# A two-layer decoder trunk in split fp32: the down projections as seven products of halves, the residual kept with tokens on the partitions

## The chip, the cores and the metric

One Trainium2 chip, one of its cores. The metric is the device time of one launch in microseconds (us); lower is better. The kernel before takes 1899.91 us, the median of 3 runs (1899.79 to 1900.06).

## The reference

Two layers, each a feed-forward part, a mixing part and a second feed-forward part, on 512 tokens of width 1024, in float32:

```python
D_MODEL = 1024; SEQ = 512; DEPTH = 2; D_FF = 2816
POOL_WINDOWS = (2, 4, 8, 16)     # four pool groups of 128 channels
HEAD_DIM = 64; N_Q_HEADS = 8; N_KV_HEADS = 2; WINDOW = BLOCK = 128

def swiglu(h, w_gu, w_down):
    g, u = jnp.split(h @ w_gu, 2, axis=-1)
    return (jax.nn.silu(g) * u) @ w_down

for l in range(DEPTH):
    x = x + 0.5 * swiglu(rmsnorm(x, ln_ffn1[l]), w_ffn1_gu[l], w_ffn1_down[l])
    h = rmsnorm(x, ln_mix[l])
    u_pool, q, k, v, gate_logits = jnp.split(h @ w_in[l], splits, axis=-1)
    a = pool_mixer(u_pool, pool_w[l], pool_scale[l]) @ w_pool_branch[l]
    b = swa_sink_attention(rope(norm(q)), rope(norm(k)), v, sinks[l]) @ w_attn_branch[l]
    g_pool, g_attn = jnp.split(jax.nn.sigmoid(gate_logits), 2, axis=-1)
    x = x + (g_pool * a + g_attn * b) @ w_out[l]
    x = x + 0.5 * swiglu(rmsnorm(x, ln_ffn2[l]), w_ffn2_gu[l], w_ffn2_down[l])
```

## The kernel before

**Arithmetic.** Every operand of a large product is split into a high part of type fp32r and a rest (`hi`, `lo`), and a product is three matmuls: hi with hi, hi with lo, lo with hi (`term`). The function `split` makes the pair: ScalarE (ACT) copies with rounding, VectorE (DVE) subtracts. Weights come in chunks of up to 1024 columns (`raw`, seven buffers) by DMA; `W.prep` is called after each half product and makes `wh` (ACT) and `wl` (DVE) of chunks ahead of use, up to four (`HI`) and three (`LO`) chunks ahead. All instructions run in the order in which the program writes them, on each engine: `keep_in_program_order`. All of them are issued from one helper line, so the profile gives one line number, L95, for nearly everything, and groups are told apart by the names of their tiles.

**A feed-forward part (`ffn`).** The 2816 hidden columns are 22 tiles of 128, in three groups of 8, 8 and 6 tiles. A group is two blocks of gate and up products (`block`, 512 or 384 columns of each) and then its part of the down product (`down`). A block forms its gate and up by seven products of half size in place of eight, named a11, s1, s2, s3, a12, s4, a22 after the weights they use; the weights move, the activations (`xgh`, `xgl`, in the combinations B11, T1 to T4, B21, B22) are stationary. Sums of weights come from accumulating DMAs on GpSimd's queue and from DVE (`sums`). Results `r` (first half of the tokens) and `v` (second half) have tokens on the partitions; `turned` transposes them on TensorE (PE) and splits them into the hidden operand `hh`, `hl`. The very first block (`plain`) uses no such products.

**Down, before.** For each of the eight output tiles `m` of 128 columns, the weights are stationary and the hidden operand moves: 8 (or 6) hidden tiles by 3 matmuls of 512 columns into one PSUM bank; `done` adds half of it to the residual `x`, held with features on the partitions (`[128, 8, 512]`). In the last group of a part, `done` also feeds the next norm: `nxt.split(m)` and `nxt.square(m)`. The norm's factor is applied behind the product (`rstd`), from a sum of squares that four matmuls with a column of ones (`sums`) form; in the mixing part it is spread over all partitions as `R`.

**The mixing part (`mix`).** It computes u (the pool input), q, k, v, the gates and the two branches, then `out`, again tile by tile with features on the partitions. Short chains of DVE, ACT and PE work (pool windows, the attention of the heads) are `stages` that run between the large products at places listed in tables (`NORMS`, `HEADS`, `ATT`, `POOL`).

**PSUM, before.** Eight banks of 512 columns. Each accumulator is a tile of one bank: six for the blocks and the down products, `pt_tp` and `pt_pv` for transposes; in `mix` four for products and a pair for scores.

Of the kernel before, what the change touches and what calls it, by code (L numbers as in the profile page):

```python
# [28 lines left out]
HALVES = (0, 4, 1, 5, 2, 6, 3, 7)  # L29
# [77 lines left out]
def trunk(ctx, tc, xT, consts, vecs, rows, w_g4, w_g3, w_d8, w_d6, w_qkv, w_u, w_pool, w_gate, w_br, w_out, out):  # L107
# [12 lines left out]
    x = xp.tile([P, KT, S], F32, name="x")  # L120
# [7 lines left out]
    pw = pa.tile([P, S], F32, name="pt_pv")  # L128
    for _ in range(WARM):
        nc.tensor.matmul(pw[:, :2 * P], warm[:, :P], warm, start=True, stop=True)  # L130
# [26 lines left out]
    class Weights:  # L157
# [3 lines left out]
        def __init__(self):  # L161
# [3 lines left out]
            for l in range(L):  # L165
                for f in range(2):
                    if f == 1:
                        for kind, src, n in (("u", w_u[l], 2), ("qkv", w_qkv[l], 6), ("u", w_u[l, 2:], 2),
                                             ("gate", w_gate[l], 2 * KT), ("br", w_br[l], KT)):
                            for i in range(n):  # L170
                                self.add(kind, CH, src[i])
                        for m in HALVES:
                            self.add("out", CH, w_out[l, m])
                    plain = l == f == 0
                    for gi, (at, group) in enumerate(groups(plain)):
                        for i, n in enumerate(group):
                            w = w_g4[l, f, (at - 768) // 512 + i] if at else w_g3[l, f, i]
                            if plain and gi == i == 0:
                                for j in range(2):
                                    for c in range(4):  # L180
                                        self.add("plain", 2 * n, w[j, c])
                            else:
                                self.block(w, 2 * n, FIRST if 2 * gi + i == int(plain) else ORDER)
                        for m in (HALVES if f == 1 and gi == 2 else range(KT)):
                            w = w_d8[l, f, at // 1024, m] if at else w_d6[l, f, m]
                            self.add("dn", sum(group), w)
# [8 lines left out]
        def block(self, w, n, order):  # L195

            at, name, first = len(self.plan), {}, len(self.loads)
            src = {"a11": (w[0], None), "s1": (w[1], w[1, 2:]), "s3": (w[0], w[1]), "a12": (w[0, 2:], None),
                   "a22": (w[1, 2:], None), "s2": (None, None), "s4": (None, None)}
            for k in order:  # L200
                for c in range(2):
                    s, m = src[k]
                    name[k, c] = self.add(k, n, None if s is None else s[c], None if m is None else m[c])
# [108 lines left out]
    bank = {}  # L312

    def mm():
        return bank["mm"].tile([P, S], F32, name="mm")
# [16 lines left out]

    class Norm:
# [5 lines left out]
        def split(self, k, between=lambda: None):  # L339

            g = self.gain[:, k:k + 1]
            if self.h is None:
                self.h = xl.tile([P, 7 * 4 * HT], F32R, name="xgh")
                self.l = xl.tile([P, 7 * 4 * HT], F32R, name="xgl")
                self.spare = [t[:, KT * S:] for t in (self.h, self.l)]
                if self.halves:
                    self.h, self.l = (t.rearrange("p (i k t) -> p i k t", i=7, k=4) for t in (self.h, self.l))
                else:
                    self.h, self.l = (t[:, :KT * S].rearrange("p (k t) -> p k t", k=KT) for t in (self.h, self.l))
            if not self.halves:  # L350
                split(self.h[:, k, :], self.l[:, k, :], x[:, k, :], scale=g, between=between)
            elif k < 4:
                split(*self.of(B11, k), halves(x[:, k, :])[:, 0:1, :], scale=g, between=between)
                self.first(k)
            else:
                xg = self.scaled(k)
                bh, bl = self.of(B21, k - 4, 2)
                nc.scalar.copy(out=bh, in_=halves(xg))
                between()
                self.others(k - 4, xg, lambda: nc.vector.tensor_tensor(  # L360
                    out=bl, in0=halves(xg), in1=bh.bitcast(F32), op=ALU.subtract
                ))

        def of(self, i, j, n=1):
            return [t[:, i:i + n, j, :] for t in (self.h, self.l)]

        def scaled(self, k):
            xg = temp("xg")
            nc.scalar.activation(out=xg, in_=x[:, k, :], func=AF.Copy, scale=self.gain[:, k:k + 1])
            return xg  # L370

        def first(self, j):
            d = temp("d")[:, :HT]
            nc.vector.tensor_tensor(out=d, in0=x[:, j, :HT], in1=x[:, j, HT:], op=ALU.subtract)
            split(*self.of(T1, j), halves(d), scale=self.gain[:, j:j + 1])

        def others(self, j, xg, between=lambda: None):
            t, u = temp("t23"), temp("t4")[:, :HT]
            gj = self.gain[:, j:j + 1]
            nc.vector.scalar_tensor_tensor(  # L380
                out=t[:, HT:], in0=x[:, j, HT:], scalar=gj, in1=xg[:, HT:], op0=ALU.mult, op1=ALU.subtract
            )
            nc.vector.scalar_tensor_tensor(
                out=t[:, :HT], in0=x[:, j, :HT], scalar=gj, in1=t[:, HT:], op0=ALU.mult, op1=ALU.subtract
            )
            nc.vector.tensor_tensor(out=u, in0=xg[:, :HT], in1=t[:, :HT], op=ALU.subtract)
            between()
# [3 lines left out]
        def split_plain(self, k, b12):  # L391
            g = self.gain[:, k:k + 1]
            if self.h is None:
                self.h, self.l = (
                    xl.tile([P, 7 * 4 * HT], F32R, name=n).rearrange("p (i k t) -> p i k t", i=7, k=4)
                    for n in ("xgh", "xgl")
                )
            if k < 4:
                split(*self.of(B11, k), halves(x[:, k, :])[:, 0:1, :], scale=g)
                split(*(t[:, k:k + 1, :] for t in b12), halves(x[:, k, :])[:, 1:2, :], scale=g)  # L400
            else:
                split(*self.of(B21, k - 4, 2), halves(x[:, k, :]), scale=g)

        def square(self, k):
            if self.acc is None:
                self.acc = xp.tile([P, S], F32, name="ssq")
                nc.scalar.activation(out=self.acc, in_=x[:, k, :], func=AF.Square)
            else:
                sq = temp("sq")
                nc.scalar.activation(out=sq, in_=x[:, k, :], func=AF.Square)  # L410
                nc.vector.tensor_tensor(out=self.acc, in0=self.acc, in1=sq, op=ALU.add)

        def sums(self, pt=None):
            if pt is None:
                pt = pa.tile([P, S], F32, name="pt_tp")
            for b in range(NB):
                nc.tensor.matmul(
                    pt[:, b:b + 1], self.acc[:, b * P:(b + 1) * P], ones[:, 0:1], start=True, stop=True
                )
            v = sp.tile([P, NB], F32, name="rs_v")  # L420
            nc.vector.tensor_scalar(
# [4 lines left out]
            if self.halves:  # L426
                return
# [7 lines left out]
        def spread(self):  # L435
            pr = pa.tile([P, S], F32, name="pt_pv")
# [8 lines left out]

    @with_exitstack
    def ffn(ctx, nm, nxt, last):
        hp = ctx.enter_context(tc.tile_pool(name="hp", bufs=1, reuse_waits="tile"))
        ep = ctx.enter_context(tc.tile_pool(name="ep", bufs=1, reuse_waits="tile"))
        sums = ctx.enter_context(tc.tile_pool(name="sums", bufs=2, reuse_waits="tile"))  # L450
        bank["mm"] = ctx.enter_context(tc.tile_pool(name="pf", bufs=6, space=PSUM, reuse_waits="tile"))
# [9 lines left out]
        turns = []  # L461

        def block(n, base, hid, order):
# [3 lines left out]
            pt = {}  # L467

            def product(i, b, kind, go):
                first = b not in pt  # L470
                if first:
                    pt[b] = [mm()[:, :n] for _ in range(2)]
                for c in range(2):
                    wh, wl = (t[:, :2 * n].rearrange("p (k f) -> p k f", k=2) for t in W.take(kind))
                    for q in range(2):
                        for k in range(2):
                            ah, al = (t[:, i, 2 * c + k, q * P:(q + 1) * P] for t in (nm.h, nm.l))
                            for j, (s, m) in enumerate(((ah, wh), (ah, wl), (al, wh))):
                                nc.tensor.matmul(
                                    pt[b][q], s, m[:, k, :], start=first and c == k == j == 0,  # L480
                                    stop=c == k == 1 and j == 2, skip_group_check=True,
                                )
                    if c == 0:
                        W.prep()
                if kind == order[1]:
                    turn()
                after = go() if go else None
                if kind == order[0]:
                    turn()
                W.prep()  # L490
                if after:
                    after()

            def each(make):
                return [make(q) for q in range(2)]

            new = lambda name: [ep.tile([P, 512], F32, name=f"{name}{q}")[:, :n] for q in range(2)]
            r1, sa, u2, v = {}, {}, {}, {}
# [561 lines left out]
```

## Time and profile before

| | before |
|---|---|
| median of 3 runs (lowest to highest) | 1899.91 us (1899.79 to 1900.06) |
| the profiled execution, from first to last instruction | 1899.3 us |
| PE matmul busy | 1890.0 us, 9072 matmuls |
| DVE busy | 1293.7 us |
| ACT busy | 840.3 us |
| GpSimd (POOL) busy | 83.1 us |
| moved by DMA | 256.10 MB |

The page lists, for each engine, the time in which an instruction ran; matmuls overlap, so that their busy times say little of how tightly they follow one another. For that the chain of waits and the timeline serve, where each row gives a start. The span is one execution under the profiler; what lies around it is the 0.6 us by which the median of the runs is longer.

### The profile page before, as it was taken

To read this page: it belongs to the slowest core of one execution; us is meant where nothing else is said; L and a number is where in the kernel's file an instruction comes from. 1 tells how busy PE (TensorE), PEld (TensorE's weight loads), DVE (VectorE), ACT (ScalarE), POOL (GpSimd) and SP (SyncE) were. 2 spreads that over 40 slices of the span, in tenths; PEclk is the share of its full clock that TensorE was granted. 3 is DMA by queue.
4 is the path that set the end of the run, shared out by engine and by line. 5 is a ranking of instruction groups with operands and counts; after the bars stand their busy time and mean duration, and the time that the engine had idled before them with its cause. 6 is when DMAs were issued, how large, how long until landed. Compare 5 with 4: busy or idle time off the path is not lost.

```text
span 1899.3 us, 23841 instructions
## 1 busy us (share of the span) xinstructions
PE 1890.0 (100%) x9072; PEld 1596.5 (84%) x9072; DVE 1293.7 (68%) x1897; ACT 840.3 (44%) x1269; POOL 83.1 (4%) x104
## 2 busy tenths in 40 slices
PE   9999999999999999999999999999999999999999
PEld 8988888887788889988888898888877888899887
DVE  7768476576667865767787485865675688567683
ACT  6435254346445542435554253443554454334351
POOL 0000000000000000000000000000000000000000
PEclk9999999999999999999999999999999999999999
DMA  7665564322224654565465466632222247455651
GB/s 205 177 174 159 133 167 133 106 89 67 78 89 111 189 145 129 161 176 161 130 171 156 104 167 167 181 117 95 89 67 89 91 109 211 128 144 161 166 156 45
DMA packets 76626, 256.10 MB, mean 135 GB/s; under 512 B 8640, under 2 KB 8896, under 8 KB 76512
## 3 DMA queue, kind: packets, MB, share of 16 engines
q1 hardware_dynamic: 63072, 209.84, 34.7%
q0 software_dynamic: 13296, 44.71, 13.8%
q8 instruction: 71, 1.16, 0.3%
q14 instruction: 43, 0.35, 0.1%
q10 hardware_dynamic: 144, 0.03, 0.0%
HBM read 252.45 MB, written 2.10 MB: 134 GB/s over the span
## 4 chain that ended last, share of the span: by engine, by line
PE 95%; DVE 3%; ACT 2%; issue 0%; DMA 0%; SPq 0%; ACTq 0%; DVEq 0%
PE mm L95 89%; PE sc L95 2%; PE pt_pv L95 2%; PE pt_tp L95 2%; DVE wl L95 1%; ACT s L95 0%; ACT wh L95 0%; ACT xgh L95 0%; DVE hss L95 0%; DMA x<-in_xT 0%; DVE win L95 0%; DVE xgl L95 0%; DVE t L95 0%; DVE d L95 0%; DVE m L95 0%
## 5 line engine op out<-in xcount | busy, mean ns | idle before, releaser
L95 ACT CAST wh<-raw 128x1024 fp32r<-128x1024 f32 (+2 forms) x419 | 414.8, 990 | 498.6 <-PE mm L95 450.5
L95 DVE TENSOR_TENSOR wl<-raw,wh 128x1024 fp32r<-128x1024 f32 (+2 forms) x419 | 479.6, 1147 | 115.9 <-PE mm L95 74.5
L95 PE MATMUL mm<-wh,xgh 128*128 128x512 f32 (+2 forms) x1392 | 517.3, 372 | 0.7 <-ACT wh L95 0.7
L95 PE MATMUL mm<-wl,xgh 128*128 128x512 f32 (+2 forms) x1392 | 515.2, 370 | 2.4 <-DVE wl L95 2.2
L95 PE MATMUL mm<-wh,xgl 128*128 128x512 f32 (+2 forms) x1392 | 514.9, 370 | 0.0
L95 PEld LDWEIGHTS mm<-wl,xgh 128*128 128x128 f32 x1392 | 261.5, 188 | 39.8 <-DVE wl L95 4.2
L95 PEld LDWEIGHTS mm<-wh,xgh 128*128 128x128 f32 x1392 | 261.5, 188 | 37.3 <-ACT wh L95 1.3
L95 PEld LDWEIGHTS mm<-wh,xgl 128*128 128x128 f32 x1392 | 261.4, 188 | 36.4
L95 PE MATMUL mm<-hh,wh 128*128 128x512 f32 x704 | 276.2, 392 | 0.0
L95 PE MATMUL mm<-hh,wl 128*128 128x512 f32 x704 | 274.2, 389 | 0.0
L95 PE MATMUL mm<-hl,wh 128*128 128x512 f32 x704 | 273.9, 389 | 0.0
L95 DVE SCALAR_TENSOR_TENSOR x<-mm,x 128x512 f32<-128x512 f32 x96 | 66.3, 691 | 199.7 <-PE mm L95 199.7
L95 ACT CAST wh<-sums 128x1024 fp32r<-128x1024 f32 (+1 forms) x92 | 90.9, 988 | 165.7 <-PE mm L95 85.4
L95 PEld LDWEIGHTS mm<-hh,wl 128*128 128x128 f32 x704 | 132.1, 188 | 27.6
L95 PEld LDWEIGHTS mm<-hl,wh 128*128 128x128 f32 x704 | 132.2, 188 | 26.7
L95 PEld LDWEIGHTS mm<-hh,wh 128*128 128x128 f32 x704 | 132.2, 188 | 26.7
L95 POOL DMA_DIRECT2D raw<-in_w_g x92 | 79.4, 863 | 1713.8 <-DMA raw<-in_w_g 1024.3
L95 PE MATMUL mm<-xgh,wh 128*128 128x512 f32 x384 | 153.9, 401 | 0.0
L95 PE MATMUL mm<-xgl,wh 128*128 128x512 f32 x384 | 150.0, 391 | 0.0
L95 PE MATMUL mm<-xgh,wl 128*128 128x512 f32 x384 | 149.9, 390 | 0.0
L95 DVE TENSOR_TENSOR wl<-sums,wh 128x1024 fp32r<-128x1024 f32 (+1 forms) x92 | 104.1, 1138 | 12.9 <-PE mm L95 12.9
L95 PEld LDWEIGHTS mm<-xgh,wh 128*128 128x128 f32 x384 | 72.1, 188 | 20.1 <-issue 5.6
(211 smaller groups left out, 1933.7 us busy)
## 6 DMA issues: line engine op xcount, KB each, us to landing
raw<-in_w_g SPq DMA_DIRECT2D x160, 512.0 KB, 4.3
raw<-in_w_g POOLq DMA_DIRECT2D x64, 512.0 KB, 7.2
raw<-in_w_d SPq DMA_DIRECT2D x64, 512.0 KB, 3.6
raw<-in_w_g SPq DMA_DIRECT2D x77, 384.0 KB, 3.5
raw<-in_w_gate SPq DMA_DIRECT2D x32, 512.0 KB, 3.4
raw<-in_w_d SPq DMA_DIRECT2D x32, 384.0 KB, 3.2
raw<-in_w_g POOLq DMA_DIRECT2D x28, 384.0 KB, 5.8
raw<-in_w_br SPq DMA_DIRECT2D x16, 512.0 KB, 3.4
```

The costliest lines, as they stand in the source:

```text
L95: return lambda *args, **kw: self.tc.keep_in_program_order(call(*args, **kw))
```

## The change

- `down` is formed as a block is: token halves, halves of the group's hidden tiles (the two blocks) and halves of the 1024 output columns, seven products in place of eight. The weight columns move and the hidden operand `op` is stationary. `turned` makes `op` from the transposes of the blocks' results, with sums and differences in `fa`, `fb`, `fc`.
- The residual `x` has tokens on the partitions (`[128, 4, 1024]`). It is loaded a second time in that form, the output is written in that form, and `out` moves weight columns too.
- Each norm's input comes from `feed(k, pt)`: four transposes of a 128-column strip of `x` into PSUM, then gain and split from there. Strips 0 to 3 are fed inside the last product of the part before; 4 to 7 and the combinations `others` are queued in `pend` and drawn by `due` inside the first products of the next part. The sum of squares is taken by ACT with `accum_out` (`squares`), without matmuls.
- PSUM becomes four tiles of two banks: `mm0`, `mm1`, `mm2`, which take the roles A, C and Dd in turn, and `pt` (`turn`). Evacuations read both banks in one instruction. `mm()` hands out halves of the two-bank tiles.
- The order of the seven products changes (`ORDER`, `FIRST`).

```diff
-ORDER = ("a11", "s2", "s1", "s3", "a12", "s4", "a22")
-FIRST = ("a11", "a12", "s2", "s1", "s3", "s4", "a22")
+ORDER = ("a11", "s1", "s2", "a12", "s3", "s4", "a22")
+FIRST = ("a11", "s1", "a12", "s2", "s3", "s4", "a22")
...
-    x = xp.tile([P, KT, S], F32, name="x")
+    x = xp.tile([P, NB, D], F32, name="x")
...
+    two = [pa.tile([P, 2, S], F32, name=f"mm{i}") for i in range(3)]
+    turn = pa.tile([P, 2, S], F32, name="pt")
...
     def mm():
-        return bank["mm"].tile([P, S], F32, name="mm")
+        ring[0] += 1
+        i = (ring[0] - 1) % 4
+        return roles[1 - i // 2][:, i % 2, :]
...
+        def feed(self, k, pt):
+            self.opened()
+            for b in range(NB):
+                nc.tensor.transpose(pt[:, b * P:(b + 1) * P], x[:, b, k * P:(k + 1) * P], ident)
             g = self.gain[:, k:k + 1]
             if not self.halves:
-                split(self.h[:, k, :], self.l[:, k, :], x[:, k, :], scale=g, between=between)
+                split(self.h[:, k, :], self.l[:, k, :], pt, scale=g)
+                return
...
+            A, C, Dd = roles
+            bank = {"a11": A, "s2": A, "s3": A, "a22": A, "s1": C, "s4": C, "a12": Dd}
...
+        def turned(src, i, t, n):
+            jn = n // P
+            for q in range(2):
+                for j in range(jn):
+                    nc.tensor.transpose(turn[:, q, j * P:(j + 1) * P], src[:, q, j * P:(j + 1) * P], ident)
+            pt = turn[:, :, :n]
...
+            elif t == 1:
+                nc.vector.scalar_tensor_tensor(
+                    out=f["a"], in0=f["a"], scalar=-1.0, in1=pt, op0=ALU.mult, op1=ALU.subtract
+                )
+                f["c"] = fp.tile([P, 2, S], F32, name="fc")[:, :, :n]
+                nc.scalar.copy(out=f["c"], in_=pt)
+                made("s2", f["a"], n)
+                nc.vector.tensor_tensor(out=f["b"], in0=pt, in1=f["b"], op=ALU.subtract)
...
-            for m in ms[3:]:
-                pd = mm()
-                part(pd, W.take("dn"), range(kts))
-                done(m, pd)
+            def a11(pt):
+                add(0, 0, 0.5)(pt)
+                return flush
...
+                mid["a22", 0, 1] = lambda: [nxt.feed(i, Dd[:, i, :]) for i in range(2)]
+                mid["a22", 1, 1] = lambda: [nxt.feed(2 + i, turn[:, i, :]) for i in range(2)]
+                pend.extend(stages(nxt, [A[:, 0, :], A[:, 1, :], turn[:, 0, :], turn[:, 1, :]]))
```

**Place 1: DVE, from the end of a group's second block into its down product.** Here `r` is the block's result for the first half of the tokens, `pt` the transposes on their way, `wl` and `sums` weight work. Before:

```order
L95 TENSOR_TENSOR r_1453<-mm,r_1453 128x512
L95 TENSOR_TENSOR r_1454<-mm,r_1454 128x512
L95 SCALAR_TENSOR_TENSOR r_1453<-r_1453,rstd,sa_1631 128x512
L95 SCALAR_TENSOR_TENSOR r_1454<-r_1454,rstd,sa_1632 128x512
L95 TENSOR_TENSOR wl<-raw,wh 128x1024
L95 TENSOR_TENSOR hl<-pt_tp,hh 128x4x128
L95 TENSOR_TENSOR hl<-pt_pv,hh 128x4x128
```

Now, from the same place:

```order
L96 SCALAR_TENSOR_TENSOR r_1412<-mm_95,nrstd,r_1412 128x512 x2
L96 TENSOR_TENSOR wl<-raw,wh 128x1024
L96 TENSOR_TENSOR sums<-raw 128x1024
L96 SCALAR_TENSOR_TENSOR fa<-fa,pt 128x1024
L96 TENSOR_TENSOR op<-fa,op 128x1024
L96 TENSOR_TENSOR fb<-pt,fb 128x1024
L96 TENSOR_TENSOR wl<-raw,wh 128x1024
L96 TENSOR_TENSOR sums<-raw 128x1024
L96 SCALAR_TENSOR_TENSOR x<-mm_93,x 128x2x512
```

The two subtractions that made `hl` from two separate tiles have become three instructions on the one tile `pt`, behind two pieces of weight work. On PE the transposes of `r` into that tile stand behind the first down product, which is 24 matmuls on the bank pair `mm_93`; the last rows of that product and the first behind it are:

```order
L96 MATMUL mm_93<-wh,op 128x512 x2
L96 MATMUL mm_93<-wl,op 128x512
L96 MATMUL mm_93<-wh,op 128x512
L96 MATMUL pt<-cst,r_1412 128x128 [waits DVE_49]
L96 MATMUL pt<-cst,r_1412 128x128 x7
L96 MATMUL mm_94<-wh,op 128x512 [waits Activation_49]
```

**Place 2: PE, the last down product of a part, where the next norm is fed.** Before, no transposes stood there. Now two strips of `x` go into the two halves of `mm_93`:

```order
L96 MATMUL mm_93<-cst,x 128x128 [waits DMAHW2_49]
L96 MATMUL mm_93<-cst,x 128x128 [waits DMAHW3_49]
L96 MATMUL mm_93<-cst,x 128x128 [waits DMAHW4_49,DVE_49]
L96 MATMUL mm_93<-cst,x 128x128 [waits DMAHW5_49]
L96 MATMUL mm_93<-cst,x 128x128 [waits DVE_49]
L96 MATMUL mm_93<-cst,x 128x128 x3
L96 MATMUL mm_95<-wh,op 128x512 [waits Activation_49]
L96 MATMUL mm_95<-wl,op 128x512
```

The fifth row is the first transpose of the second strip: it has a wait on DVE of its own, though it writes the other half.

**Place 3: PE in `mix`, a pool window's product (`dh`, `dl` with `xgh` or `th`) inside the first u product.** Before:

```order
L95 MATMUL mm<-xgh,wl 128x512
L95 MATMUL mm<-dh,xgh 128x512 [waits Activation_49]
L95 MATMUL mm<-dl,xgh 128x512 [waits DVE_49]
L95 MATMUL mm<-dh,xgl 128x512
L95 MATMUL mm<-xgh,wh 128x512
L95 MATMUL mm<-xgl,wh 128x512
```

Now:

```order
L96 MATMUL mm_93<-xgh,wl 128x512
L96 MATMUL mm_93<-dh,th 128x512 [waits Activation_49]
L96 MATMUL mm_93<-dl,th 128x512 [waits DVE_49]
L96 MATMUL mm_93<-dh,tl 128x512
L96 MATMUL mm_93<-xgh,wh 128x512 [waits DVE_49]
L96 MATMUL mm_93<-xgl,wh 128x512
```

The running product shares the two-bank tile with the window's product, and its next matmul has got a wait on DVE.

More of the change, by code (lines that the diff above doesn't have):

```diff
@@ L182, in __init__ @@
                             else:
[L183 to L186, printed above, removed]
+                                src = lambda h, k, c, w=w: w[h, 2 * k + c]
+                                self.block(src, (2 * n, 2 * n), FIRST if 2 * gi + i == int(plain) else ORDER)
+                        if at:
+                            w = w_d8[l, f, at // 1024]
+                            self.block(lambda h, k, c, w=w: w[h, k, c], (CH, CH), ORDER)
+                        else:
+                            w = w_d6[l, f]
+                            cols = slice(0, CH), slice(CH, 3 * S)
+                            self.block(lambda h, k, c, w=w: w[h, k][:, cols[c]], (CH, S), ORDER)
         def add(self, kind, n, src=None, more=None, of=None):
@@ L330, in rsqrt @@
             nc.vector.scalar_tensor_tensor(out=y, in0=t, scalar=1.5, in1=y, op0=ALU.add, op1=ALU.mult)
+    parts = [xp.tile([P, 2, NB], F32, name=f"part{i}") for i in range(2)]
     class Norm:
@@ L364, in of, with opened @@
[L364 to L372, printed above, removed]
+            self.part = parts[0]
+            parts.reverse()
+        def opened(self):
+            if self.h is None:
+                self.h, self.l = (xl.tile([P, KT * S], F32R, name=n) for n in ("xgh", "xgl"))
+                shape = dict(i=4, k=4) if self.halves else dict(k=KT)
+                form = "p (i k t) -> p i k t" if self.halves else "p (k t) -> p k t"
+                self.h, self.l = (t.rearrange(form, **shape) for t in (self.h, self.l))
+                self.more, self.keep = {}, {}
@@ L392, in split_plain @@
             g = self.gain[:, k:k + 1]
[L393 to L397, printed above, removed]
+            self.opened()
             if k < 4:
-                split(*self.of(B11, k), halves(x[:, k, :])[:, 0:1, :], scale=g)
-                split(*(t[:, k:k + 1, :] for t in b12), halves(x[:, k, :])[:, 1:2, :], scale=g)
-            else:
-                split(*self.of(B21, k - 4, 2), halves(x[:, k, :]), scale=g)
@@ L404, in square @@
[L404 to L407, printed above, removed]
+                split(*self.of(B11, k), halves(src)[:, 0:1, :], scale=g)
+                split(*(t[:, k:k + 1, :] for t in b12), halves(src)[:, 1:2, :], scale=g)
+            else:
+                split(*self.of(B21, k - 4, 2), halves(src), scale=g)
+        def square(self, k, src, acc):
+            if k == 0:
+                nc.scalar.activation(out=acc, in_=src, func=AF.Square)
@@ L408, in square @@
             else:
                 sq = temp("sq")
[L410 to L419, printed above, removed]
-            v = sp.tile([P, NB], F32, name="rs_v")
+                nc.scalar.activation(out=sq, in_=src, func=AF.Square)
@@ new lines, in square, with squares, sums @@
+                nc.vector.tensor_tensor(out=acc, in0=acc, in1=sq, op=ALU.add)
+        def squares(self, d, b):
+            nc.scalar.activation(
+                out=temp("sq"), in_=x[:, b, d * S:(d + 1) * S], func=AF.Square, accum_out=self.part[:, d, b:b + 1]
+            )
+        def sums(self, acc=None, pt=None):
+            v = sp.tile([P, NB], F32, name="rs_v")
+            if acc is not None:
+                for b in range(NB):
+                    nc.tensor.matmul(pt[:, b:b + 1], acc[:, b * P:(b + 1) * P], ones[:, 0:1], start=True, stop=True)
+            else:
+                pt = v
+                nc.vector.tensor_tensor(out=v, in0=self.part[:, 0, :], in1=self.part[:, 1, :], op=ALU.add)
@@ L492, in product @@
                     after()
[L494 to L498, printed above, removed]
-            rs = lambda b: nm.rstd[:, b:b + 1]
-            def p1():
-                r1.update(enumerate(new("r")))
-                each(lambda q: nc.scalar.copy(out=r1[q], in_=pt[1][q]))
+            roles[:] = [Dd, C, A]
+        rs = lambda b: nm.rstd[:, b:b + 1]
@@ L504, in p1, with block @@
+        nrs = lambda b: nm.nrstd[:, b:b + 1]
+        count = [0]
+        def block(n, i, order, mid):
+            count[0] += 1
+            r = wide(f"r{count[0] % 2}")[:, :, :n]
+            tile_ = {}
+            def a11(pt):
+                nc.scalar.copy(out=r, in_=pt)
                 if W.sums is None:
                     open_sums()
-            def p2():
-                if nm.rstd is not None:
-                    gate()
-            def gate():
-                sa.update(enumerate(new("sa")))
-                each(lambda q: nc.scalar.activation(out=sa[q], in_=pt[1][q], func=AF.Silu, scale=rs(q)))
@@ L565, in turn, with s2, a12 @@
-        def turn():
-            for t in turns[:2]:
-                turned(*t)
-            turns[:2] = []
-        def plain(n, base, hid):
+            def s2(pt):
+                tile_["u"] = wide("u")[:, :, :n]
+                for q in range(2):
+                    nc.scalar.copy(out=tile_["u"][:, q, :], in_=pt[:, q, :])
+            def a12(pt):
+                nc.vector.tensor_tensor(out=r, in0=r, in1=pt, op=ALU.add)
+                for q in range(2):
+                    nc.scalar.activation(out=r[:, q, :], in_=r[:, q, :], func=AF.Silu, scale=rs(q))
@@ L573, in plain, with flush @@
+        def flush():
+            if turns:
+                turned(*turns.pop(0))
+        def plain(n, xt, acc, later):
             b12 = [sums.tile([P, 4 * HT], F32R, name="sums").rearrange("p (k t) -> p k t", k=4) for _ in range(2)]
-            whole = [mm() for _ in range(6)]
-            pts = [t[:, :n] for t in whole]
+            part = lambda k: xt[k // 4][:, k % 4, :]
+            A, C, Dd = roles
             for k in range(KT):
-                nm.split_plain(k, b12)
+                nm.split_plain(k, b12, part(k))
@@ L662, in ffn @@
                 else:
-                    block(n, base, hid, FIRST if W.sums is None else ORDER)
-                base += n // P
-            final = gi == 2
-            if final:
-                W.sums = None
-            down(hid, base, final, HALVES if final and nxt is not None and nxt.halves or final and last else list(range(KT)))
+                    starts = W.sums is None
+                    mid = {}
+                    if nm is first and starts:
+                        mid["s1", 1, 1] = flush
+                    elif starts:
+                        mid = {("a11", 0, 1): lambda: due(2), ("a11", 1, 1): lambda: due(2), ("s1", 0, 1): due,
+                               ("s1", 1, 1): due, ("a12", 0, 1): due, ("a12", 1, 1): due}
@@ L671, in mix, with stages, one @@
+                    block(n, i, FIRST if starts else ORDER, mid)
+            down(n, gi == 2)
+    def stages(nm, pts):
+        xg = {}
+        def one(k, pt):
+            xg[k] = nm.feed(k, pt)
+        out = [lambda k=k, pt=pt: one(k, pt) for k, pt in zip(range(4, KT), pts)]
+        if nm.halves:
+            out += [lambda j=j: nm.others(j, nm.keep[j], xg[j + 4]) for j in range(4)]
+        return out
     @with_exitstack
@@ L918, in mix @@
             if not q:
-                split(wph, wpl, praw)
+                for g in range(len(WIN)):
+                    split(*part_of(g, slice(S, S + P)), praw[:, g * P:(g + 1) * P])
             side(-1 if q else -3)
```

490 lines of the change are left out of this document (292 added, 198 removed).

## The prediction

> **What bounds the kernel now.** The page comes first: is there one engine that never rests, and does its clock hold?
>
> ```profile
> span 1899.3 us, 23841 instructions
> PE 1890.0 (100%) x9072; PEld 1596.5 (84%) x9072; DVE 1293.7 (68%) x1897; ACT 840.3 (44%) x1269; POOL 83.1 (4%) x104
> ...
> PEclk9999999999999999999999999999999999999999
> ...
> PE 95%; DVE 3%; ACT 2%; issue 0%; DMA 0%; SPq 0%; ACTq 0%; DVEq 0%
> ```
>
> PE is busy for the whole span at full clock, and the chain that ended last runs through it for 95%. Busy time counts overlapped matmuls, so the second view is the list of PE's waits; this is its largest group:
>
> ```profile
> PE mm L95 <- DVE wl L95: 2.2, 4, 1.1
> ```
>
> Four waits, the longest 1.1 us: PE is fed all through. So the time is the number of matmuls times their cadence, and the chain in order of time gives that. These rows are a block's end and its down product:
>
> ```profile
> 311.80 5.46 PE mm L95 x24
> 317.26 0.44 PE pt_tp L95 x4
> ...
> 318.14 43.54 PE mm L95 x192
> 361.67 0.79 PE pt_tp L95 x8
> ```
>
> 43.54 / 192 = 0.2268 us for a matmul of 512 columns; 24 of them, which is one half-size product, 5.46; a 128x128 transpose 0.11; a norm's sums (the last row) 0.79. The last view is the busy time by windows (us, then PE, PEld, DVE, ACT, POOL, clock, DMA share, GB/s), a block first, a down product second, in each pair (512 columns wide, then 384):
>
> ```profile
> 662.00:700.00 38.00, 38.00 (x178) 31.64 (x177) 28.52 (x33) 17.21 (x20) 0.86 (x1) 1.00 0.53 148
> 702.00:740.00 38.00, 38.00 (x171) 31.76 (x171) 15.53 (x18) 7.55 (x8) 2.62 (x3) 1.00 0.43 104
> 774.00:802.00 28.00, 28.00 (x160) 27.36 (x159) 22.59 (x33) 13.85 (x20) 0.80 (x1) 1.00 0.49 151
> 806.00:836.00 30.00, 30.00 (x134) 24.85 (x133) 16.76 (x19) 8.61 (x9) 1.72 (x2) 1.00 0.71 178
> ```
>
> DVE works 28.5 of 38 us in a block and rests in the down product (15.5). The average of 68% hides that: down is where DVE catches up today, and where the change puts new work.
>
> **What PE saves.** Seven products for eight: a group of 8 hidden tiles goes from 8 x 8 x 3 = 192 to 7 x 24 = 168 matmuls, a group of 6 from 144 to 126. Two large and one small group in four feed-forward parts: 4 x (24 + 24 + 18) = 264 fewer, x 0.2268 = **-59.9**. Five norms need 32 transposes each: 160 x 0.109 = **+17.4**. Their matmuls for the sums go: 5 x 0.79 = **-4.0**. Net **-46.5**, certain as long as PE is never kept waiting. `out` moves weights instead of activations at the same count: nothing.
>
> **What the others pay.** These are the prices, by group (mean ns behind the comma):
>
> ```profile
> L95 DVE TENSOR_TENSOR wl<-raw,wh 128x1024 fp32r<-128x1024 f32 x308 | 374.9, 1220 | 91.7 <-PE mm L95 53.9 <-PE sc L95 20.4 <-issue 17.3
> L95 DVE TENSOR_TENSOR wl<-raw,wh 128x768 fp32r<-128x768 f32 x109 | 103.5, 953 | 24.2 <-PE mm L95 20.6 <-issue 3.2 <-ACT wh L95 0.4
> L95 ACT CAST wh<-raw 128x1024 fp32r<-128x1024 f32 x308 | 322.8, 1048 | 373.3 <-PE mm L95 332.4 <-PE sc L95 24.6 <-issue 4.7
> L95 DVE SCALAR_TENSOR_TENSOR x<-mm,x 128x512 f32<-128x512 f32 x96 | 66.3, 691 | 199.7 <-PE mm L95 199.7
> L95 DVE TENSOR_TENSOR sums<-raw 128x1024 f32<-128x1024 f32 x32 | 38.8, 1219 | 0.0
> L95 ACT COPY r<-mm 128x512 f32<-128x512 f32 x32 | 18.0, 587 | 23.2 <-PE pt_tp L95 16.6 <-PE mm L95 6.7
> ```
>
> A DVE instruction over two banks (1024 columns) stands in no row. Below, it can't be under the 0.69 of 512 columns; above, two of those make 1.38. I take 1.2, the 1.22 of 1024 columns without PSUM; likewise 1.0 for ACT's copy over two banks (0.59 to 1.17). In a 512-wide down DVE now has 14 `wl`, 4 `sums`, 6 additions to `x`, and 8 instructions for `op`, `fa`, `fb`, all 1024 wide, and two of 512: 32 x 1.2 + 2 x 0.69 = 39.8 us, where PE has 168 x 0.2268 + 16 x 0.109 = 39.8. DVE is as long as PE there, with no slack to absorb a queue. The additional accumulating DMAs (48 more on POOL's queue) lie beside a DMA share of 0.43 to 0.71 and cost nothing; without that cover each would delay one chunk of weights. The second load of `x` and the output's rows have the same cover, or the same place at the end.
>
> **Term 1: the flush inside each down.** The transposes of `r` go into the tile `pt` behind the first down product (place 1). They must wait for the last reader of the earlier transposes, `fb<-pt,fb`. Count from the last matmul of the block. For the handover I use this pair from the timeline:
>
> ```profile
> 421.24 0.39 PE L95 MATMUL mm<-xgh,wl 128*128 128x512 f32 x1
> ...
> 421.66 0.69 DVE L95 TENSOR_TENSOR z<-mm,R 128x512 f32<-128x512 f32 x1 [2.41 <-PE mm L95]
> ```
>
> A reader starts 0.42 us after the start of the last matmul, 0.2 after its share of 0.2268. Then, in DVE's order: `r` twice (to 1.6), `wl` (2.8), `sums` (4.0), `fa` (5.2). ACT's `fc` reads the same tile and has a wait on DVE's `fa`: to 6.2; its cast of `op` to 7.2; DVE subtracts `op` (8.45) and makes `fb` (9.65); PE may go on at 9.8. PE meanwhile has 8 transposes (0.88) and one product (5.46): 6.3. It stands **3.5 us**. As DVE can't catch up inside the down, I add 0.8 to 0.9 for a second, smaller wait at s4, whose operand comes from `fc`: 4.3 for each of 8 wide downs; for the 4 narrow ones the same chain with 768 columns ends at 8.3 against 4.7 (6 transposes and 18 matmuls), 3.6 and a lag of 1.4: 5. 8 x 4.3 + 4 x 5 = **+54**. Bounds: 28, if one of `wl` and `sums` is done earlier and s4 doesn't wait (12 x 2.3); 72, if two-bank reads take 1.38 and the lag doubles (12 x 6).
>
> **Term 2: the feeds.** Two strips go into the two halves of one tile, and the order shows that the second's transposes wait for the first's readers (place 2).
>
> ```profile
> L95 ACT ACTIVATE xgh<-x,vec 128x512 fp32r<-128x512 f32 x20 | 14.4, 722 | 45.7 <-DVE x L95 45.7
> L95 DVE SCALAR_TENSOR_TENSOR xgl<-x,vec,xgh 128x512 fp32r<-128x512 f32 x20 | 14.9, 747 | 0.0
> L95 ACT ACTIVATE xg<-x,vec 128x512 f32<-128x512 f32 x16 | 11.6, 726 | 26.2 <-DVE x L95 26.2
> L95 DVE SCALAR_TENSOR_TENSOR t<-x,vec,t 128x256 f32<-128x256 f32 x16 | 7.8, 485 | 0.6
> L95 DVE TENSOR_TENSOR t<-xg,t 128x256 f32<-128x256 f32 x16 | 6.8, 425 | 0.6
> ```
>
> Into `mix` the readers are ACT's `xgh` and, behind it, DVE's `xgl`: 0.2 + 0.72 + 0.75 + two handovers, about 1.9 bare. Four pairs: 1.9 twice, 2.5 and 3.1 where DVE is behind with weights, and 0.5 more at a handover between pairs: 9.8 for each of two norms, **+19.6**. Into a feed-forward part the reader is ACT's copy alone: 0.2 + 0.73 + 0.2 = 1.1; the norm behind `mix` has 1.1, 1.9, 1.1 (4.1, twice), the one behind the first layer 1.8 + 2.3 + 2.9 + 2.3 + 1.1 = 10.4, since ACT and DVE there come out of a full down: **+18.6**. Bounds of both: 24 (bare chains) and 45.
>
> **Term 3: the first block of a part.** `others` costs DVE, for one strip, two rows of 0.485, one of 0.425, and splits of 0.75 and 0.42: 2.6; four strips 10.3, all before the weights that stand behind them. A product of 5.46 needs 2 x 1.2 for its `wl`: s2's chunk comes 5.2 late, with two later waits of 0.9. And in the new `FIRST` s2 and s3 follow each other on the same pair of banks, so that s3 waits for ACT's two copies (1.6 bare, 4.0 behind ACT's queue). 5.2 + 1.8 + 4.0 = 11.0 for each norm behind `mix`; behind the first layer 0.3 + 4.9 + 1.6 + 4.3 = 11.1: **+33**; the very first such block, with no feeds, 2: **+2**. Bounds: 14 and 45.
>
> **Term 4: shared tiles in `mix`.** A running u product now waits until the window's result in the other half has been split (place 3).
>
> ```profile
> 412.28 0.74 DVE L95 SCALAR_TENSOR_TENSOR xgl<-mm,vec,xgh 128x512 fp32r<-128x512 f32 x1
> ...
> 404.80 0.40 PE L95 MATMUL mm<-dh,xgl 128*128 128x512 f32 x1
> ```
>
> The window's last matmul starts at 404.80, and its split ends at 413.02: 8 us behind the matmul's share. Nobody waits for that now. It becomes a stall of 8.0 for the first window; the three others come to 1.7, 0 and 2.25, and gate products that wait for `z` in the neighbouring half (0.2 + 0.69, less what PE has to do) and q's transposes to 5.5: 17.5 a layer. `mix` loses 2.5 of waits that it has now: 15 x 2 = **+30**. Bounds: 18 and 40.
>
> **The sum**, against the profiled execution's 1899.3: -46.5 + 54 + 19.6 + 18.6 + 33 + 2 + 30 = +110.7, so **2010**; the runs' median lies 0.6 above the span: **2011**. With all lower bounds -46.5 + 28 + 24 + 14 + 18 = +37.5, 1937; with all upper ones -46.5 + 72 + 45 + 45 + 40 = +155.5, 2055.
>
> **Rivals.**
> - *The clock falls in the new stalls.* Today no wait exceeds 1.1 us and the clock is full, so no row shows what a stall of 4 or 8 us does. The stalls of 4 us and more add up to 2 x 8 + 2 x (5.2 + 4.0) + 4.9 + 4.3 = 43.6; if the clock is halved for as long behind each, matmuls lose half of that, 21.8: **2033**; with the 12 flushes of 3.5 another 21. The Trainium skill ("TensorE: Matmul & The Clock Gate", HAM oscillation) says that PE idle gaps above about 3.4 us bring the clock back to half; no run here shows it yet, and by its figure the flushes sit at the edge.
> - *Readers keep up in down* (the other side). Place: the flush. If weight work (`wl`, `sums`, 2.4) isn't between `r` and `fa`, and `fc` runs beside `fa` (1.0), the chain ends at 6.4, PE's 6.3 cover it and all 12 flushes are free. With shared tiles as harmless elsewhere, PE keeps its saving but for term 3: -46.5 + 4 + 33: **1890** (1853 if that goes too). It decides at a chain of 6.3 us. Against it: DVE's order puts both between, and `fc` carries a wait.
> - *Waits by half tiles.* If a wait is for the reader of the same half only, terms 2 and 4 vanish: -46.5 + 54 + 33 = +40.5, **1940**. Against it: the fifth row of place 2.
> - That the change doesn't do what it says (fewer matmuls) is excluded by the count of instructions.
>
> **How the numbers follow.** Forecast 0.65, clock 0.14, half tiles 0.10, readers keep up 0.11. A measurement of this kernel tells about 0.2% (4 us) from no change. The first three end slower, 0.89, of which 0.01 goes to a tie; the last ends faster, 0.10, and 0.01 in a tie: within 0.2% 0.02, slower 0.88. The range takes the half tiles and the bounds of the terms: 1935 to 2055; it leaves out the faster case and the far end of the clock's.
>
> **What would show it.** 6480 matmuls of 512 columns at 0.227. PE's waits on DVE (`fb`, by the row of `pt<-cst,r`) about 3.5 us in each of 12 downs; DVE over 95% busy in a down's window; two waits of about 2 us between feeds 0 and 1; a wait near 8 us behind the first window of `mix`. If the clock row shows less than 9 behind long waits, the first rival has come in. Wrong would be: PE's waits under 45 us in all (then it is faster), or waits on DMA in front of the down weights, which I priced at nothing.

## The result, and the profile after

| | before | after |
|---|---|---|
| median of 4 runs | 1899.99 us (1899.79 to 1900.55) | 2047.28 us (2043.1 to 2051.07) |
| ratio, 95% interval | | 1.0773 (1.0757 to 1.0788) |
| span of the profiled execution | 1899.3 us | 2049.3 us |

The change makes the kernel 7.7% slower. The forecast was 2011 us, range 1935 to 2055. The profiled execution of the changed kernel is the longest of its four (2051.07 us with a mean clock of 0.971; the shortest, 2043.10, has 0.976), so that sums from its trace lie some 4 us above the median. The page of the changed kernel:

```profile
span 2049.3 us, 23932 instructions
PE 1908.7 (93%) x8928; PEld 1590.7 (78%) x8928; DVE 1461.9 (71%) x1873; ACT 1001.5 (49%) x1457; POOL 124.8 (6%) x152
...
PEclk9999999989999999999989999999999999999999
...
PE 78%; DVE 13%; ACT 6%; issue 3%; DMA 0%; SPq 0%; DVEq 0%; ACTq 0%
```

There are fewer PE instructions, and the chain that ended last now runs for 19% through DVE and ACT. PE's waits (us in all, times, longest), where five microseconds stood before:

```profile
PE pt L96 <- DVE fb L96: 35.5, 12, 3.0
PE mm L96 <- DVE tl L96: 19.4, 6, 8.1
PE mm L96 <- DVE z L96: 17.7, 14, 2.3
PE mm L96 <- DVE wl L96: 17.6, 10, 4.3
PE mm L96 <- ACT u L96: 12.5, 4, 4.0
PE mm L96 <- DVE xgl L96: 8.5, 4, 2.4
PE pt L96 <- DVE xgl L96: 6.3, 4, 1.6
```

The first row is the flush in each of the 12 downs. The timeline at one of the four narrow downs (those behind blocks of 384 columns) shows its chain on DVE (768 columns), link by link; the block's last matmul ended its share 0.2 us ahead of the first row. The last two rows are ACT's links, which stand between `fa` and `op`:

```profile
1225.15 1.14 DVE L96 SCALAR_TENSOR_TENSOR r<-mm,nrstd,r 128x384 f32<-128x384 f32 x2 [0.41 <-PE mm L96]
1226.21 1.21 DVE L96 TENSOR_TENSOR wl<-raw,wh 128x1024 fp32r<-128x1024 f32 x1
1227.34 1.22 DVE L96 TENSOR_TENSOR sums<-raw 128x1024 f32<-128x1024 f32 x1
1228.48 0.95 DVE L96 SCALAR_TENSOR_TENSOR fa<-fa,pt 128x768 f32<-128x768 f32 x1
1231.02 0.96 DVE L96 TENSOR_TENSOR op<-fa,op 128x768 fp32r<-128x768 f32 x1 [1.60 <-ACT op L96]
1231.89 0.95 DVE L96 TENSOR_TENSOR fb<-pt,fb 128x768 f32<-128x768 f32 x1
...
1229.46 0.80 ACT L96 COPY fc<-pt 128x768 f32<-128x768 f32 x1 [3.64 <-DVE fa L96]
1230.15 0.83 ACT L96 CAST op<-fa 128x768 fp32r<-128x768 f32 x1
```

And PE in the same stretch:

```profile
1229.50 0.39 PE L96 MATMUL mm<-wh,op 128*128 128x512 f32 x1
1232.90 1.54 PE L96 MATMUL pt<-cst,r 128*128 128x128 f32 x6 [3.01 <-DVE fb L96]
1234.09 0.78 PE L96 MATMUL mm<-wh,op 128*128 128x512 f32 x1
1234.67 0.63 PE L96 MATMUL mm<-wl,op 128*128 128x512 f32 x1
1235.09 1.05 PE L96 MATMUL mm<-wh,op 128*128 128x512 f32 x2
...
1239.40 0.40 PE L96 MATMUL mm<-wl,op 128*128 128x512 f32 x1
```

PE stands 3.01 us for `fb`, and what follows is the second half of the loss: a matmul takes 0.63 where it takes 0.39, six transposes 1.54. The windows give the granted clock there (third number from the right); the first row is a whole wide down (512-wide blocks), with DVE's busy time behind those of PE and PEld:

```profile
757.60:799.90 42.30, 39.38 (x180) 32.40 (x179) 36.84 (x34) 18.94 (x20) 3.45 (x4) 1.00 0.59 144
...
1233.80:1238.80 5.00, 5.00 (x15) 4.03 (x14) 4.24 (x5) 1.32 (x2) 0.00 (x0) 0.50 0.75 203
1239.00:1262.00 23.00, 22.59 (x100) 18.36 (x99) 20.40 (x22) 12.07 (x15) 1.73 (x2) 1.00 0.68 180
```

The clock is 0.50 in the five microseconds shown behind the stall, and full again behind that. The same in `mix`, at the shared tile:

```profile
416.96 0.40 PE L96 MATMUL mm<-dh,tl 128*128 128x512 f32 x1
425.48 0.79 PE L96 MATMUL mm<-xgh,wh 128*128 128x512 f32 x1 [8.12 <-DVE tl L96]
426.07 0.63 PE L96 MATMUL mm<-xgl,wh 128*128 128x512 f32 x1
```

### The profile page after: what moved, and what is told of

The parts are those of the page before. It is cut to its first block, busy times and chain, and to the rows that moved or that the text cites. A ratio compares the mean times of both kernels' runs of the same rounds, so it can differ in the third digit from the quotient of the medians.

```text
span 2049.3 us, 23932 instructions
## 1 busy us (share of the span) xinstructions
PE 1908.7 (93%) x8928; PEld 1590.7 (78%) x8928; DVE 1461.9 (71%) x1873; ACT 1001.5 (49%) x1457; POOL 124.8 (6%) x152
## 4 chain that ended last, share of the span: by engine, by line
PE 78%; DVE 13%; ACT 6%; issue 3%; DMA 0%; SPq 0%; DVEq 0%; ACTq 0%
PE mm L96 75%; PE pt L96 3%; DVE wl L96 3%; DVE sums L96 1%; ACT wh L96 1%; ACT s L96 1%; DVE x L96 1%; DVE tl L96 1%; ACT xgh L96 1%; ACT op L96 1%; DVE fb L96 1%; ACT sq L96 1%; DVE fa L96 1%; ACT th L96 1%; DVE r L96 1%
## 5 line engine op out<-in xcount | busy, mean ns | idle before, releaser
L96 ACT CAST wh<-raw 128x1024 fp32r<-128x1024 f32 (+3 forms) x443 | 434.4, 988 | 352.7 <-PE mm L96 279.6
L96 DVE TENSOR_TENSOR wl<-raw,wh 128x1024 fp32r<-128x1024 f32 (+3 forms) x443 | 504.5, 1145 | 114.3 <-PE mm L96 88.1
L96 PE MATMUL mm<-wh,op 128*128 128x512 f32 x1232 | 395.4, 399 | 0.0
L96 PE MATMUL mm<-wl,xgh 128*128 128x512 f32 (+2 forms) x904 | 331.9, 367 | 2.0 <-DVE wl L96 1.9
L96 PE MATMUL mm<-wh,xgl 128*128 128x512 f32 (+2 forms) x904 | 331.7, 367 | 0.0
L96 PEld LDWEIGHTS mm<-wh,op 128*128 128x128 f32 x1232 | 237.5, 193 | 49.6
L96 PE MATMUL mm<-wl,op 128*128 128x512 f32 x616 | 244.8, 397 | 1.6 <-DVE wl L96 1.6
L96 PE MATMUL mm<-wl,th 128*128 128x512 f32 (+1 forms) x552 | 211.3, 383 | 14.1 <-DVE wl L96 14.1
L96 PE MATMUL mm<-wh,th 128*128 128x512 f32 (+1 forms) x552 | 211.3, 383 | 12.8 <-ACT u L96 12.5
L96 PE MATMUL mm<-wh,tl 128*128 128x512 f32 (+1 forms) x552 | 210.3, 381 | 0.0
```

Of the source, the lines that this page charges most:

```text
L96: return lambda *args, **kw: self.tc.keep_in_program_order(call(*args, **kw))
```

## The experiments

Three theories: PE's waits come from tiles of two banks; the clock falls because PE idles; and DVE has no slack in a down, so that a wait there moves when it is taken away. All runs are compared with the kernel before (1900 us), by medians; "the change" is 2047.

**1. The flush one product later.**

```diff
             def a11(pt):
                 add(0, 0, 0.5)(pt)
-                return flush
             def s1(pt):
                 add(1, 1, -0.5)(pt)
                 made("s3", f["b"], n)
+                return flush
```

> The flush of the block's result stands behind the second down product in place of the first; nothing else is changed. Theory (PE stands 3.1 us in each of 12 downs because the chain up to fb is longer than one product, and the half-clock stretches behind those stalls cost another 12 us in sum): the 12 waits on fb (37.5 us) go, the stretches with them, and no new wait of over 1 us takes their place: 2049 - 37 - 12, about 2000 us (1990 to 2010). Rival (DVE has as much work in a down as PE, so the stall only moves to a later wait on DVE): within 10 us of the changed kernel, 2037 or more.

Measured: 2036.69 us, ratio 1.0718 (1.0702 to 1.0734). The waits on `fb` are gone, but another group has grown from 17.6 us in 10 waits:

```profile
PE mm L96 <- DVE wl L96: 45.0, 39, 4.3
```

35 us of waits became 27 of others, about 1 us each. Those are too short for the clock: it is 0.982 in the mean against 0.971, with 15 slow stretches in the trace where the change has 25, and the gain of 11 us comes from there. The rival holds for the stall, and the time lies at the edge of its band; the theory holds for the clock behind the stall alone, and its 1990 to 2010 are missed.

**2. The stall filled.** PE gets matmuls to do in place of the wait; nothing else moves.

```diff
...
+                    idle = roles[2][:, 0, :]
+                    for _ in range(13):
+                        nc.tensor.matmul(idle, ops["a11"][:, 0, 0, 0:P], held["w"][:, 0:S], start=True, stop=True)
                     flush()
```

> Ahead of the flush in each of the 12 downs PE does 13 matmuls of 512 columns (2.95 us) into a bank that is free there, and whose result is overwritten; the wait on fb is filled and not removed. Theory (the clock falls because PE idles): the wait on fb shrinks to about 0.2 us, the matmuls behind it run at full cadence, the mean clock rises by about 0.006 and the time falls by about 12 us, to 2035. Rival (the clock falls by the chip's load or at random, not by the idle time): same number of slow stretches behind the flush, time unchanged or up by some us.

Measured: 2039.82 us, ratio 1.0735 (1.0718 to 1.0753), mean clock 0.979. PE at the place shown above:

```profile
1223.29 3.33 PE L96 MATMUL mm<-wh,op 128*128 128x512 f32 x14
1226.69 0.87 PE L96 MATMUL pt<-cst,r 128*128 128x128 f32 x6
1227.32 0.47 PE L96 MATMUL mm<-wh,op 128*128 128x512 f32 x1
1227.63 0.39 PE L96 MATMUL mm<-wl,op 128*128 128x512 f32 x1
```

And the window behind the filled stall:

```profile
1226.80:1232.00 5.20, 5.20 (x27) 4.38 (x28) 5.20 (x7) 2.65 (x4) 0.00 (x0) 1.00 0.78 175
```

With 156 matmuls more the kernel is 7 us faster. The transposes take 0.87 in place of 1.54, the clock stays at 1.00, and no slow stretch follows any of the 12 flushes. So it is the idling that costs the clock, not load or chance. The size was 7 where 12 had been expected; 12 had been taken from the profiled execution, the longest of four, and between the two profiled executions it is 12.7.

**3. One-bank tiles in `mix`.**

```diff
...
-        return roles[1 - i // 2][:, i % 2, :]
+        return single[(ring[0] - 1) % 4]
...
+        pm = ctx.enter_context(tc.tile_pool(name="pm", bufs=1, space=PSUM, reuse_waits="tile"))
...
+                    got[j] = pm.tile([P, S], F32, name=f"m{j}")
...
```

> The mixing part opens PSUM tiles of its own: six of one bank and one of two for the scores; the feed-forward part keeps its four tiles of two banks. Theory (waits come from tiles that span two banks, of which PE waits for the reader of the other half): the 8 us waits behind the window's split (19.8 us in all), those on z (some 20 us), and those between strips 4 to 7 in front of the mixing part (about 9 us) go, and the slow stretches behind them (about 17 us): 2049 - 65, about 1985 (1975 to 2000). Rival (those chains of DVE and ACT are late for themselves, and PE would need their results anyway): at most 20 us faster, 2030 or more.

Measured: 1979.10 us, ratio 1.0417 (1.0401 to 1.0432): 68 us faster. Waits on `tl` and `z` have left the list, whose first rows are now:

```profile
PE pt L96 <- DVE fb L96: 35.8, 12, 3.0
PE mm L96 <- DVE wl L96: 17.9, 10, 4.4
PE mm L96 <- ACT u L96: 12.4, 4, 4.0
```

DVE runs the same number of instructions (1873) for the same busy time (1460.7 us in place of 1461.9); what has changed is who waits for whom. The edit also gives the transposes of strips 4 to 7 ahead of `mix` tiles of their own, and their waits on `xgl` fall from 14.8 to 6.8 us; those are a part of the 68. No other single edit gained as much.

**4. The strips of a pair in different tiles.**

```diff
-                mid["a22", 0, 1] = lambda: [nxt.feed(i, Dd[:, i, :]) for i in range(2)]
...
+                mid["a22", 0, 1] = lambda: [nxt.feed(i, t[:, 0, :]) for i, t in enumerate((Dd, turn))]
...
```

> The two strips of a pair are transposed into different tiles (Dd and pt, A and pt) in place of the two halves of one. Theory: the waits of the second strip, 31 us in all at present, fall to under 10, since the reader of a tile has a whole half product before the tile is written again; with the slow stretches behind them about 25 us faster, 2023 (2015 to 2030). Rival (the readers are the bound, DVE and ACT being behind with weights, so that the matmuls that need the strips wait instead): within 8 us.

Measured: 2025.41 us, ratio 1.0658 (1.0642 to 1.0673): 22 us faster. As the theory has it: the waits on `xgl` (14.8 us) and on `xg` (5.6) have left the list.

**5. Less work for DVE in a down.** First by moving the additions of weights (with experiment 1's edit):

```diff
-                    nc.vector.tensor_tensor(
+                    nc.gpsimd.tensor_tensor(
                         out=c["raw"][:, :n], in0=a["raw"][:, :n], in1=b["raw"][:, :n], op=ALU.add
```

> As flush_late, and the additions of weights (sums) run on GpSimd in place of DVE: DVE gives up 4 of its 32 instructions of 1024 columns in a down. Theory (in a down DVE has as much work as PE, and the 39 waits on wl, 45 us in flush_late, are this lack of slack): they fall under 20 us and the time by 20 to 35, to 2002 to 2017. Rival (GpSimd is much slower at such an addition, and the chunks made from its sums come late, or its traffic slows DVE): no gain over flush_late's 2037, with waits on ACT's wh<-sums or longer DVE rows.

Measured: 2173.57 us, ratio 1.1433 (1.1416 to 1.1451). Groups by form (mean ns behind the comma):

```profile
L96 POOL TENSOR_TENSOR sums<-raw 128x1024 f32<-128x1024 f32 x52 | 140.6, 2704 | 0.0
L96 DVE TENSOR_TENSOR wl<-raw,wh 128x1024 fp32r<-128x1024 f32 x344 | 491.2, 1437 | 103.9 <-PE mm L96 66.6 <-issue 27.7 <-ACT wh L96 9.0
```

An addition takes 2.7 us there against 1.22 on DVE, and DVE's own subtractions went from 1221 ns (in flush_late) to 1437 on average: the load came back as slowness. This says nothing on DVE's slack, so the additions of the downs were left out instead:

```diff
+                    if not c["down"]:
                         nc.vector.tensor_tensor(
...
+                    elif a["of"] is None:
+                        nc.scalar.copy(out=c["raw"][:, :n], in_=a["raw"][:, :n])
```

> As flush_late, but the additions of weights for the down products s2 and s4 are left out: DVE does none of the 4 in a down, ACT copies 2 chunks instead (these two products use a11's weights). Theory (DVE has no slack in a down, so the 39 waits on wl of flush_late, 45 us, are its load): with 28 in place of 32 instructions (35 us of PE's 39.8) those waits fall under 20 us, the time to 2000 to 2015. Rival (the waits come from the short ring of three low chunks and from ACT's cast ahead of each subtraction, whatever DVE's load): over 2027.

Measured: 1998.04 us, ratio 1.0515 (1.0500 to 1.0531), 39 us below flush_late, and the group that had taken over is back where it was:

```profile
PE mm L96 <- DVE wl L96: 17.9, 10, 4.3
```

Four of 32 instructions decide it. Leaving out an addition also takes a link out of the way from `raw` to `wl`, but DVE's trace speaks for the load: in each of the 12 downs of flush_late DVE works without a rest of over 0.15 us for 22 us (narrow) to 27 us (wide) from the start of `fb` on, so that no single link holds it up; in late_nosums the first such rest comes after 20 to 22.

**6. The first blocks' order.** The closing product of a first block is formed here ahead of s3's part, which it lacks; so it is in joined and joined_pool.

```diff
-FIRST = ("a11", "s1", "a12", "s2", "s3", "s4", "a22")
+FIRST = ("a11", "s1", "a12", "s2", "s4", "s3", "a22")
```

> In the first block of a part s4 stands ahead of s3 (FIRST = a11, s1, a12, s2, s4, s3, a22), so that s2 and s3 no longer follow each other on one pair of banks; s3 and a22 do instead. Theory (s3 waits for ACT's copies of s2's result, 12.5 us in the profile): these waits go and a22 waits about 1.4 us for DVE's addition in their place; with the slow stretches behind them 8 to 13 us faster, 2034 to 2039. Rival (ACT is behind there, and every later product inherits it): within 4 us of 2047.

Measured: 2046.23 us, ratio 1.0764 (1.0746 to 1.0782): nothing gained. The 12.5 us on `u` are gone, and these 10.9 stand in their place:

```profile
PE mm L96 <- ACT th L96: 5.5, 3, 2.0
PE mm L96 <- DVE p L96: 5.4, 4, 1.4
```

The rival holds: ACT and DVE are behind in those blocks, whatever the order.

**7. All together**, and what is left.

> mix_banks, feeds_apart on the feed-forward side (a free bank pair for the third strip), flush_late and first_order together; DVE's work is unchanged. Theory (the waits are separate and add up): 2047 less 68 (mix_banks, measured), 11 (flush_late, measured), some 14 of the feeds that mix_banks leaves and 10 of first_order: about 1944 (1935 to 1955), slower than the kernel before by 2 to 3%. Rival (each wait that goes leaves the next one longer, because DVE is the bound of the downs and of the first blocks): over 1960.

Measured: 1951.02 us, ratio 1.0265 (1.0250 to 1.0280), mean clock 0.991: within the band of the theory. The waits are separate, except for `wl` in the downs, which has 47.3 us in 42 waits. With GpSimd's additions:

> joined, with the additions of weights on GpSimd. Theory (what is left is DVE's load): 1944 less 20 to 35, 1909 to 1924, with the clock above 0.99. Rival (GpSimd's additions are late or slow DVE): as joined or slower.

2088.17 us, ratio 1.0971 (1.0926 to 1.1015), as late_pool lets one expect. Two attempts at the queue ahead of `wl` follow. They, and the last version, form the first blocks' closing product behind s3's part; no run has that alone, so that the distance to joined contains it:

```diff
-RAW = 7
-HI, LO = 4, 3
+RAW = 6
+HI, LO = 4, 4
...
```

> joined (with the closing product of a first block put behind s3, so that s3's part is in it), and a fourth buffer for low chunks (LO 4, HI 4), for which one of seven raw buffers is given up. Theory (DVE is short in the downs only, and has 10 of 38 us to spare in the blocks): weights made one chunk earlier take up the queue in part, the 47 us of waits on wl fall to 20 to 35, 1951 to about 1930. Rival (six raw buffers delay the loads, or DVE is short everywhere): 1950 or more, with waits on DMA.

1989.18 us, ratio 1.0469 (1.0451 to 1.0486). No wait on DMA, and those on `wl` are gone from the head of the list; PE waits for `x`, `th` and `p` instead, 58 us in all: DVE now stands in front of ACT's `wh` (336.6 us of its waits), which has no chunk of lead left, and its other work comes late.

```diff
...
-                after = steps[kind](pt[:, :, :n])
                 W.prep()
+                after = steps[kind](pt[:, :, :n])
...
```

> joined (closing product as in joined_ahead), with the weight work of a product's end put ahead of the reading of its result, in blocks and downs. Theory (PE waits for wl since three to five instructions that nobody waits for soon stand ahead of it): waits on wl fall under 25 us, 1951 to 1925 to 1940. Rival (the results are then late, and the next writer of the bank or the transposes wait for them): 1950 or more, with waits on x, r or u in place of wl.

1956.90 us, ratio 1.0296 (1.0281 to 1.0312): the waits on `wl` fall to 26.6 us, and those on `x`, `th` and `p` rise to 34. In both the time is the rival's, 1950 or more, though the first has none of the waits on DMA that its rival named: order moves the wait about, it doesn't remove it. Last, whether the seven products would pay if DVE had room:

> joined (closing product as in joined_ahead) without the additions of weights for the downs (as in late_nosums: s2 and s4 of the downs use a11's weights). It asks whether the seven products would pay if DVE had room in the downs. Theory (the rest is separate): 1951 less the 39 that late_nosums showed, about 1912 (1905 to 1920), still slower than the kernel before, since the first blocks' waits and the clock behind them remain. Rival (with DVE's queue short, the first blocks' waits and the slow stretches go too): under 1895, faster than before.

1915.56 us, ratio 1.0077 (1.0061 to 1.0094). Even so it is 0.8% slower than the kernel before, and the theory holds. No version found here beats the kernel before (the best that leaves nothing out is joined_prep with 1956.90); whether a lighter way of making the split operands would, wasn't tried.

## Why the prediction was right, and where its sizes were off

From the starts of successive matmuls, the distance above the form's usual cadence summed (single distances of over 0.15 us as stalls; runs of three or more at about half cadence apart). The two spans differ by 150.0 us, of which the rows account for 148.9:

| term | predicted | measured |
|---|---|---|
| fewer matmuls, more transposes | -46.5 | -47.0 |
| 1 flush in the downs | +54 | +39.8 |
| 2 feeds | +38.2 | +31.2 |
| 3 first blocks | +35 | +28.4 |
| 4 `mix`, less its waits of before | +30 | +42.9 |
| half clock behind stalls | 0 | +42.9 |
| single short waits, rest | 0 | +10.7 |
| sum | +110.7 | +148.9 |

- **PE's saving** came as counted.
- **The flush** was right in mechanism and order: `r`, `wl`, `sums`, `fa`, ACT's `fc` and `op`, then `op` and `fb`, in the rows shown. For the narrow down the chain was put at 8.3 us; it ended 7.9 behind the block's last matmul (1232.84 against 1224.96). By the starts of the matmuls the stall was 3.1 each, not 3.5; the lag of 0.8 to 1.4 put on top for s4 was 0.2 on average. A two-bank read costs DVE 1.22 us, where 1.2 was taken:

```profile
L96 DVE SCALAR_TENSOR_TENSOR x<-mm,x 128x1024 f32<-128x1024 f32 x72 | 87.8, 1219 | 19.2 <-PE mm L96 19.2
```

- **DVE over 95% busy in a down** was too strong: 36.84 of 42.30 us in the wide down shown, 87%, where 39.8 us of work had been counted; in the chain it waits for ACT. That it has no slack behind the chain all the same is shown by experiments 1 and 5.
- **Feeds and first blocks** came out about a fifth below their sizes.
- **`mix`** was under-sized. The first window's 8.0 us came to 8.12, but the waits on `z` (17.7 us in 14) and on q's transposes were put at 5.5 a layer together and took about twice that.
- **The clock** is the step that failed: the forecast put it at nothing, and it took 43 us. It was a rival at 0.14, at 22 us for stalls of over 4 us, with the flushes "at the edge" for 21 more. The forecast argued from a kernel without stalls, which can't show what a stall does. The rival had the direction right; that its 22 and 21 add up to the 43 measured is luck. By the clock's own record the change has 25 slow stretches, and all matmuls within them lose 46 us: 16 behind the eight stalls of over 3.5 us, 15 behind 8 of the 12 flushes, and 15 behind nine stalls of 1.6 to 2.4 us, which the rival put at nothing.
- The Trainium skill ("TensorE: Matmul & The Clock Gate", HAM oscillation) gives the rule that PE must have no idle gaps above about 3.4 us. By that rule the flushes of 3.0 us would have been safe; 8 of the 12 in the profile were not.
- **The range** held partly by luck. Flush, feeds and first blocks came out 28 us below their sizes in sum, which hid half of the 54 us of the two rows that had been put at nothing.
- The rivals **half tiles** and **readers keep up** are refuted by the waits on `tl` and on `fb`.

## What to carry to other kernels

When PE is fed without a gap, price a new stall twice: once for its length, and once for the clock behind it. Where waits are kept by tile, a tile over two accumulators makes the writer of each wait for the reader of the other; here one-bank tiles in `mix` were worth 68 us, more than the 47 that the seven products save. And an algorithm that takes work from the bound engine must be charged at the place where it puts work on the others, not by their average: DVE's 68% before hid that it rested in the downs, and those rests are what the change uses up.

## What the runs showed of the hardware that wasn't expected

- The clock is granted in steps of 3.41 us. Each of the 25 slow stretches of the change starts on one grid of 3.413 us (to within 1 ns) and lasts one, two or three of its steps. Whether a step is slow goes by how long PE idled in the step before it. In the 13 profiles of the change and its variants, of 7002 steps at full clock with under 1.5 us idle none was followed by a slow one; of 120 with 1.5 to 2.0 us, 39 were; of 193 with more than 2.0 us, all (idle by the profile's rows, in which the ends of matmuls are modelled). So a flush of 3 us costs the clock when most of it falls into one step, as in the first two rows below (2.41 us idle, then clock 0.50), and doesn't when the grid cuts it in two, as in the last two (1.60 and 1.32 us idle). Counted by single stalls, those of 0.8 to 1.5 us were followed by three or more matmuls at half cadence in about 5% of 297 cases, those of 2.0 to 3.5 us in 129 of 177, and those of 3.5 us and more in 86 of 90.

```profile
81.81:85.22 3.41, 1.00 (x8) 0.97 (x9) 2.88 (x4) 1.44 (x2) 0.85 (x1) 1.00 0.59 183
85.22:88.63 3.41, 3.41 (x10) 2.64 (x9) 3.41 (x5) 1.32 (x2) 0.00 (x0) 0.50 0.84 214
194.44:197.85 3.41, 1.81 (x9) 1.16 (x7) 1.39 (x2) 2.90 (x3) 0.00 (x0) 1.00 0.89 300
197.85:201.27 3.42, 2.09 (x14) 1.88 (x14) 3.42 (x4) 0.00 (x0) 0.86 (x1) 1.00 0.53 79
```

- GpSimd's additions of two arrays in SBUF didn't slow DVE's subtractions evenly, though the mean (1437 ns) reads so. Of the 344 subtractions of that group in late_pool, the 294 that overlapped no such addition took 1217 ns in the mean, and the 50 that did 2730. The 14 additions to `x` of the same size, which read one operand in PSUM, that overlapped one took 1211 to 1225. GpSimd ran its additions in only 16% of the span.
